# One PSUM layout for a whole two-layer block, kept rows and a turn moved in the Fourier stage, and queries turned in fp32r

## The chip, the core and the metric

The kernel runs on one core of one Trainium2 chip. The metric is device time in microseconds (us) of one execution. The time before is the median of three runs; beside it stands one profiled execution of the same kernel, from which every duration in this document is read.

## The reference, cut to what matters

A block of two layers works on 512 latent tokens of width 1024 (and, in the first layer, 256 context tokens). All of it is fp32.

- Each layer is: half-step SwiGLU FFN, a token mixer, half-step SwiGLU FFN. Every sub-layer first modulates its input (`x * (1 + scale) + shift`, from a conditioning vector) and ends with `layer_norm(ALPHA * x + gate * y) * g + b`.
- The mixer of layer 0 is attention with 16 query heads on 4 key heads of 64 columns, rotary positions, a band of 128 tokens to both sides, all context keys and one sink logit per head in the softmax.
- The mixer of layer 1 is a two-dimensional Fourier transform (over the 512 tokens, and over groups of 256 channels), its real part, and a projection.
- The context goes through the first FFN of layer 0 alone, and is used as keys and values.

```python
q, k, v = split(h @ w_qkv + b_qkv);  q, k = rope(q * scale), rope(k)
p = softmax([q k_window, q k_context, sink])          # per head, block of 128 queries
y = (p[window] @ v_window + p[context] @ v_context) @ w_o        # layer 0
y = real(fft2(h per channel group, axes=(token, channel))) @ w_o  # layer 1
x = layer_norm(ALPHA * x + gate * y) * g + b
```

## The kernel before

**Precision.** A product of two fp32 matrices is made of three products in fp32r, a 4-byte format of fewer mantissa bits. `split` (line 160) makes two parts of a matrix: `hi`, a rounded copy (ScalarE), and `lo`, what is left (VectorE). `mm3` (line 164) issues hi·hi, lo·hi and hi·lo into one PSUM accumulation. So each weight tile of 128x1024 costs a copy on ScalarE and a subtraction on VectorE (`wh`, `wl` in the profile), and for the weights whose output is gated also a product with the gate row (`wr<-wr,gr`).

**Buffers.** SBUF has a pool of 42 slots of 4 KB per partition (`slot`, line 135): weight rows as they land (`wr`), their parts, activations, probabilities, the LayerNorm rows. DMAs for weights go out on SyncE's queue, in order, as soon as a slot is free for them. PSUM has 8 banks of 512 fp32 columns. In the FFNs and the Fourier stage they are one pool of eight single banks (`open_banks(8)`); `bank` (line 144) takes one, and `bank2` (line 150) takes two of them. For the core of attention that pool is closed and another is opened, with four single banks and two tiles of two neighbouring banks (`open_banks(4, 2)`); afterwards that is closed and the eight come back. A tile of PSUM is given out again when the last instruction that reads it is through.

**Order.** TensorE and GpSimd run in the order in which the code emits. VectorE and ScalarE do so in the stretches between `nc.pin(True)` and `nc.pin(False)`; elsewhere a planner of the compiler orders their instructions. SyncE's DMAs are ordered by that planner too.

**An FFN half step** (`half_step`, line 566) runs 22 up pairs (`ffn_up`, line 410): for each, 48 matmuls into one `bank2`, a silu of one bank on ScalarE and a product with the other on VectorE. VectorE also folds the modulation vectors of later stages there (`mr`, `acc`), whose sums go through a single bank (`mp`). Then `project` (line 476) runs the down product into four `bank2` named `y`, one for each 128 tokens: the first part goes through the contraction for all four tiles together, and the last contraction tiles (`TAIL` = 4) go tile by tile, so that one token tile is finished after another. After each: `norm_stage` (VectorE), `scale_stage` (ScalarE), and for the tile before it `flip_stage` (line 351), eight turns of 128x128 on TensorE into a `bank2` named `tp`, then the affine part and the split of the next stage's input. The last tile's turns are left for the next stage, which calls them (`rest[0]`, the function `flip`) between its first products. The other function that `project` returns, `keeps` (line 533), makes the next residual: it loads two LayerNorm rows by DMA (`ln_rows`) and computes x·g + b for a token tile (`keep_stage`, line 389: two VectorE instructions of 128x1024).

**Attention** (line 925). `group` (line 1018) makes a product of 256 tokens by 512 columns into a `bank2` named `qkv`: three groups for keys and values, two for the first half of the queries, two for the second. Keys are turned by `kv_flip`. Queries of a group go through `q_post` (line 999): the bias for both token tiles (`qb`), then for each tile the rotary steps (`ra`) and `q_parts`, which puts each head's rounded part and its remainder side by side (`q`). `q_flip` (line 1006) turns them, eight 128x128 turns a token tile in fp32 into a `bank2` named `qt`, and ScalarE copies them out as `Q`. This happens eight times: four between the groups, four in steps 3 to 6 of the core. Between the last two groups, `whole` makes the scores of steps 0 and 1 with single banks. The core has 16 steps (key head by query tile); each makes the scores `s` of the step after next, turns probabilities (`pt`), and multiplies with values (`o`). A score tile has 512 or 640 columns; in the core it is one tile of two neighbouring banks. After the core the first product of `project` needs the split of the attention output (`uh`, `ul` from `oT`).

**Fourier** (line 1245). For each of four token tiles, two products `ab` of 12 matmuls of 258 columns go into one `bank2` each, and are split (`ah`, `al`) with an extra column copied to `nyq`. The turns of the last token tile of the FFN before (`rest[0]()`) are called behind both products of the second tile. Then for each of four channel groups 24 matmuls (`f`) go into two single banks, and VectorE and ScalarE combine them into `X`, which is split for the projection (`uh`, `ul`). That projection (8 contraction tiles) calls `keeps` after each of its first four contraction tiles: after the first one the rows are loaded and the first token tile is done, and so on.

L72 in the profile is the line of a helper through which all engine instructions are issued, so that groups are told apart by tile names.

Of the kernel before, what the change touches and what calls it, by code (L numbers as in the profile page):

```python
# [15 lines left out]
P = 128  # L16
# [3 lines left out]
BANK = 512  # L20
# [26 lines left out]
SLOTS = 42  # L47
EVAC_DVE = {4: (1,), 5: (1, 3)}
# [10 lines left out]
REACH_DFT = 9  # L59

# [32 lines left out]
class Banks:  # L93


    def __init__(self, tiles):
        self.tiles = tiles
# [7 lines left out]
class Emitter:  # L105
    def __init__(self, ctx, tc, ins, out):
        self.tc = tc
        self.nc = Engines(tc)
        self.ins = ins
        self.out = out  # L110
        self.pool = ctx.enter_context(tc.tile_pool(name="sb", bufs=1))
        self.dram = ctx.enter_context(tc.tile_pool(name="dram", bufs=2, space=bass.MemoryType.DRAM))
        self.open_banks(8)
        self.n = 0

    def open_banks(self, single, double=0):

        self.stack = ExitStack()
        self.psum, self.psum2 = (
            self.stack.enter_context(self.tc.tile_pool(name=nm, bufs=n, space=bass.MemoryType.PSUM)) if n else None  # L120
            for nm, n in ((f"ps{single}", single), (f"pd{single}", double))
        )
        self.bufs = single, double

    def close_banks(self):
        self.stack.close()
# [17 lines left out]
    def bank(self, nm="ps"):  # L144
        return self.psum.tile([P, BANK], F32, tag="ps", name=self.name(nm), bufs=self.bufs[0])

    def wide(self, nm):
        return self.psum2.tile([P, 2 * BANK], F32, tag="pd", name=self.name(nm), bufs=self.bufs[1])

    def bank2(self, nm="ps"):  # L150
        return Banks([self.bank(nm) for _ in range(2)])
# [4 lines left out]
    def turn(self, out, src):  # L156
        self.nc.tensor.transpose(out, src, self.ident)

# [251 lines left out]
    def ffn_up(self, pairs, h, N, quota, us, first=None, halves=False, late=None, held=None):  # L410
# [34 lines left out]
        for p in range(NPAIR):  # L445
# [10 lines left out]
            if first is not None and p in KEEP_AT:  # L456
                first[1](KEEP_AT.index(p))
# [18 lines left out]
    def project(self, w0, nf, stat, st, ntok, mid=None, keep=True, reach=REACH, each=None):  # L476
# [56 lines left out]
        def keeps(i=None):  # L533

            if keep:
                if not i:
                    st["rows"] = self.ln_rows(*st["ln"])
                for t in range(ntok) if i is None else (i,):
                    self.keep_stage(st, t)
# [61 lines left out]
    def head(self):  # L601
# [6 lines left out]
        banks = [self.bank("up") for _ in range(HEAD)]  # L608
        scratch = self.bank("ms")
        raws, xts, ws = {}, {}, {}  # L610
# [157 lines left out]
    def run(self):  # L768
# [128 lines left out]
        rest = self.project(w_fo, KC, fT, st, NT, each=keeps)  # L897
# [27 lines left out]
    def attention(self, w_kv, w_q, w_ao, h1, ch, rest):  # L925
# [52 lines left out]
        Q = {}  # L978

        def q_bias(tp, i, ps):  # L980
            qb = self.slot([P, 2, 512], F32, "qb")
            for tt in range(2):
                nc.vector.tensor_tensor(
                    qb[:, tt], ps[:, tt * 512 : (tt + 1) * 512], bq[:, i * 512 : (i + 1) * 512], ALU.add
                )
            return tp, i, qb, {}
# [5 lines left out]
        def q_parts(tp, i, qb, q2s, tt):  # L992
            q2 = self.slot([P, 8, 2, HD], F32, "q2")
            src = q2s[tt].rearrange("p (h d) -> p h d", d=HD)
            nc.vector.tensor_copy(q2[:, :, 0].bitcast(F32R), src)
            nc.vector.tensor_tensor(q2[:, :, 1], src, q2[:, :, 0], ALU.subtract)
            q2s[tt] = q2

        def q_post(tp, i, ps):
            q = q_bias(tp, i, ps)  # L1000
            for tt in range(2):
                q_rope(*q, tt)
                q_parts(*q, tt)
            return q

        def q_flip(tp, i, qb, q2s, tt):
            flip = self.bank2(nm="qt")
            for j in range(8):
                self.turn(flip[:, j * P : (j + 1) * P], q2s[tt][:, j].rearrange("p r d -> p (r d)"))
            q = self.slot([P, 8, P], F32R, "Q")  # L1010
            for h in range(2):
                src = flip[:, h * BANK : (h + 1) * BANK].rearrange("p (j q) -> p j q", q=P)
                nc.scalar.copy(q[:, 4 * h : 4 * h + 4], src)
            Q[2 * tp + tt, i] = q
# [3 lines left out]
        def group(tp, w0, last=False, between=None):  # L1018

            ps = self.bank2(nm="qkv")  # L1020
# [47 lines left out]
        def begin(n):  # L1068
# [9 lines left out]
            st = dict(g=g, b=b, total=total, nw=nw, tok=slice(b * P, (b + 1) * P))  # L1078
# [16 lines left out]
        def score(st, j):  # L1095
# [4 lines left out]
            total, nw, wide = st["total"], st["nw"], self.psum2 is not None  # L1100
# [96 lines left out]
        self.close_banks()  # L1197
        self.open_banks(4, 2)
# [40 lines left out]
        self.close_banks()  # L1239
        self.open_banks(8)  # L1240
# [4 lines left out]
    def fourier(self, w_t1, w_t2, w_fo, h, rest):  # L1245
# [11 lines left out]
        for t in range(NT):  # L1257
            pss = []
            for gp in range(FG // 2):
                ps = self.bank2(nm="ab")  # L1260
# [10 lines left out]
            if t == 1:  # L1271
                rest[0]()
            for gp in range(FG // 2):
# [5 lines left out]
                for gg in range(2):  # L1279
# [3 lines left out]
                    self.split(ah[:, t % 2, gg], al[:, t % 2, gg], src[:, : 2 * half])  # L1283
        ny = (self.slot([P, NT, P], F32R, "nyh"), self.slot([P, NT, P], F32R, "nyl"))
# [16 lines left out]
        for gr in range(FG):  # L1301
            ps, sine = (self.bank("f") for _ in range(2))
# [32 lines left out]
def kernel(ctx: ExitStack, tc: tile.TileContext, ins, out):  # L1335
    e = Emitter(ctx, tc, ins, out)
    e.run()
    e.close_banks()
# [110 lines left out]
```

## Time and profile before

| | |
|---|---|
| median of 3 runs (lowest, highest) | 1991.2 us (1990.84, 1992.42) |
| the profiled execution: its own time | 1992.59 us |
| its span, first to last instruction | 1990.8 us |
| mean granted TensorE clock | 0.999 |
| busy: TensorE, VectorE, ScalarE, GpSimd | 1971.8, 1277.0, 681.2, 73.4 us |
| DMA | 296 MB, 149 GB/s on average |
| attention up to its core | about 574 to 664 us of the span |
| the core of attention | 664 to 771 us |
| Fourier and its projection | 1548 to 1628 us |

How to read it: a group of instructions is shown by its engine and by `out<-in`, the names of the tiles. In the view of waits a line says which engine waited for which, the total, how often, and the longest. In the chain of waits each line is a start, a duration and what ran then. In the timeline a bracket behind an instruction is the time for which its engine stood idle before it, and what ended that. Records of matmuls overlap, since they are pipelined: their pace is read from their starts, or from the chain, not from their own duration.

### The profile page before, as it was taken

What the parts mean: (1) busy time and instruction counts of PE and PEld (TensorE: products, weight loads), DVE (VectorE), ACT (ScalarE), POOL (GpSimd) and SP (SyncE); (2) the same over time, 40 slices, a digit from 0 to 9 for tenths busy, and PEclk for the clock granted to TensorE, in tenths of its full rate; (3) what the DMA queues carried; (4) which work ended last, traced back from release to release, by engine and by line L of the source; (5) the groups of instructions that cost most, each with busy time, mean ns of one, the idle gap of its engine ahead of it and who ended that gap; (6) DMA issues with size and microseconds to landing.
All of it is one profiled execution on the core that took longest, in us unless ns stands there. A gap on an engine that the chain in (4) does not pass through costs nothing.

```text
span 1990.8 us, 25353 instructions
## 1 busy us (share of the span) xinstructions
PE 1971.8 (99%) x10124; PEld 1674.7 (84%) x10124; DVE 1277.0 (64%) x1713; ACT 681.2 (34%) x991; POOL 73.4 (4%) x138
## 2 busy tenths in 40 slices
PE   8999999999999999999999999999999999999998
PEld 7888888899888887988888888888888988888886
DVE  6569985598756775766658455664766873333744
ACT  3322243334533685422224232222333632212320
POOL 0000000000000460000000000000000000000000
PEclk9999999999999999999999999999999999999999
DMA  9756543388732013455543326554441333232411
GB/s 377 262 185 206 185 150 131 116 297 297 254 101 73 10 45 107 159 190 196 195 149 123 120 98 225 195 191 138 140 135 64 110 98 117 90 94 87 138 64 43
DMA packets 90198, 296.27 MB, mean 149 GB/s; under 512 B 17248, under 2 KB 17504, under 8 KB 90080
## 3 DMA queue, kind: packets, MB, share of 16 engines
q1 hardware_dynamic: 81792, 290.96, 43.0%
q10 hardware_dynamic: 8288, 3.70, 0.7%
q8 instruction: 79, 1.29, 0.3%
q14 instruction: 39, 0.32, 0.1%
HBM read 292.50 MB, written 2.13 MB: 148 GB/s over the span
## 4 chain that ended last, share of the span: by engine, by line
PE 96%; DVE 2%; DMA 1%; ACT 1%; issue 0%; DVEq 0%; POOL 0%; SPq 0%; ACTq 0%; POOLq 0%
PE up L72 54%; PE y L72 30%; PE qkv L72 4%; PE s L72 2%; PE pt L72 2%; PE o L72 1%; PE tp L72 1%; DVE wl L72 1%; DVE x L72 0%; PE ab L72 0%; DMA wr<-in_wi_head_dram 0%; PE qt L72 0%; DVE ul L72 0%; PE f L72 0%; DMA ln_b<-in_ln_b_col_dram 0%
## 5 line engine op out<-in xcount | busy, mean ns | idle before, releaser
L72 DVE TENSOR_TENSOR wl<-wr,wh 128x1024 fp32r<-128x1024 f32 (+1 forms) x359 | 429.1, 1217 | 90.9 <-ACT wh L72 55.3
L72 ACT CAST wh<-wr 128x1024 fp32r<-128x1024 f32 (+1 forms) x364 | 368.5, 1046 | 218.2 <-PE y L72 92.5
L72 PE MATMUL up<-hh,wh 128*128 128x512 f32 (+1 forms) x1152 | 429.6, 373 | 0.0
L72 PE MATMUL up<-hl,wh 128*128 128x512 f32 (+1 forms) x1152 | 428.3, 372 | 0.0
L72 PE MATMUL up<-hh,wl 128*128 128x512 f32 (+1 forms) x1152 | 428.1, 372 | 0.0
L72 PE MATMUL y<-wh,uh 128*128 128x512 f32 x920 | 302.7, 390 | 1.4 <-DVE oT L72 1.4
L72 ACT ACTIVATE sg<-up 128x512 f32<-128x512 f32 (+1 forms) x110 | 61.1, 555 | 703.5 <-PE up L72 703.5
L72 PE MATMUL y<-wh,ul 128*128 128x512 f32 x920 | 301.8, 389 | 0.0
L72 PE MATMUL y<-wl,uh 128*128 128x512 f32 x920 | 301.6, 389 | 0.0
L72 DVE TENSOR_TENSOR u<-up,sg 128x512 f32<-128x512 f32 (+1 forms) x110 | 70.1, 637 | 335.0 <-PE up L72 334.6
L72 PEld LDWEIGHTS up<-hl,wh 128*128 128x128 f32 x1152 | 217.1, 188 | 37.5
L72 PEld LDWEIGHTS up<-hh,wl 128*128 128x128 f32 x1152 | 217.2, 189 | 37.2
L72 PEld LDWEIGHTS up<-hh,wh 128*128 128x128 f32 x1152 | 217.2, 189 | 36.9
L72 PEld LDWEIGHTS y<-wh,uh 128*128 128x128 f32 x920 | 172.6, 188 | 37.1 <-DVE oT L72 1.8
L72 PEld LDWEIGHTS y<-wh,ul 128*128 128x128 f32 x920 | 172.8, 188 | 35.9
L72 PEld LDWEIGHTS y<-wl,uh 128*128 128x128 f32 x920 | 172.8, 188 | 35.5
L72 DVE SCALAR_TENSOR_TENSOR acc<-mr,silu_c,acc 128x1024 f32<-128x1024 f32 x147 | 186.1, 1280 | 1.4
L72 DVE TENSOR_TENSOR wr<-wr,gr 128x1024 f32<-128x1024 f32 x99 | 120.5, 1238 | 41.4 <-DMA wr<-in_wo_dram 22.3
L72 PE MATMUL up<-h0h,wh 128*128 128x512 f32 x352 | 139.1, 398 | 0.2 <-ACT h0h L72 0.2
L72 PE MATMUL up<-h0l,wh 128*128 128x512 f32 x352 | 136.4, 390 | 0.0
L72 PE MATMUL up<-h0h,wl 128*128 128x512 f32 x352 | 136.2, 390 | 0.0
L72 PE MATMUL up<-chh,wh 128*128 128x256 f32 x352 | 100.1, 284 | 0.0
(171 smaller groups left out, 2143.0 us busy)
## 6 DMA issues: line engine op xcount, KB each, us to landing
wr<-in_wi_dram SPq DMA_DIRECT2D x213, 512.0 KB, 4.4
mr<-in_mod_w_dram SPq DMA_DIRECT2D x144, 512.0 KB, 4.1
wr<-in_wo_dram SPq DMA_DIRECT2D x110, 512.0 KB, 3.9
m<-in_mod_head_dram SPq DMA_DIRECT2D x16, 512.0 KB, 8.1
wr<-in_wqkv_dram SPq DMA_DIRECT2D x12, 512.0 KB, 3.6
wr<-in_attn_wo_dram SPq DMA_DIRECT2D x8, 512.0 KB, 3.5
wr<-in_fourier_wo_dram SPq DMA_DIRECT2D x8, 512.0 KB, 3.5
wr<-in_wi_head_dram SPq DMA_DIRECT2D x8, 448.0 KB, 9.6
```

The lines of the kernel that those rows point to most:

```text
L72: ins = f(*args, **kw)
```

## The change

1. PSUM is divided once: four single banks (`SINGLES`) and two tiles of two neighbouring banks (`PAIRS`), from the first to the last instruction. `open_banks` and `close_banks` go. `bank2` gives a neighbouring two and two singles in turn, unless it is told which: `group` asks for a neighbouring two, `q_flip` for two singles. Steps 0 and 1 of the scores still use singles (`wide=n > 1`), now of four.
2. In `q_post` the bias, the rotary steps and the parts of one token tile are finished before the bias of the next.
3. `q_flip` turns in fp32r: the remainder is written as fp32r, and an identity in fp32r is made once by a ScalarE copy into a slot of its own. Eight flips of eight turns are concerned.
4. Fourier: the turns of the last token tile are called between the two products of the second tile instead of behind both.
5. Fourier: the LayerNorm rows are loaded behind the four token tiles, the first kept tile is computed in the first channel group, and the projection does the other three one contraction tile earlier each.

```diff
-        self.open_banks(8)
+        self.psum, self.psum2 = (
+            ctx.enter_context(tc.tile_pool(name=nm, bufs=n, space=bass.MemoryType.PSUM))
+            for nm, n in (("single", SINGLES), ("pair", PAIRS))
+        )
+        self.wide_next = True
...
-    def bank2(self, nm="ps"):
+    def bank2(self, nm="ps", wide=None):
+
+        if wide is None:
+            wide, self.wide_next = self.wide_next, not self.wide_next
+        if wide:
+            whole = self.wide(nm)
+            return Banks([whole[:, :BANK], whole[:, BANK:]], whole)
         return Banks([self.bank(nm) for _ in range(2)])
...
+    def turn_parts(self, out, src, ident):
+
+        self.nc.tensor.transpose(out.bitcast(F32R), src.bitcast(F32R), ident)
...
-                if not i:
+                if "rows" not in st:
                     st["rows"] = self.ln_rows(*st["ln"])
-                for t in range(ntok) if i is None else (i,):
+                for t in range(ntok) if i is None else i:
                     self.keep_stage(st, t)
...
-        rest = self.project(w_fo, KC, fT, st, NT, each=keeps)
+        rest = self.project(w_fo, KC, fT, st, NT, each=lambda f: keeps((f + 1,) if f + 1 < NT else ()))
...
-        def q_bias(tp, i, ps):
+        ident = self.slot([P, P], F32R, "ident_r")
+        nc.scalar.copy(ident, self.ident)
+
+        def q_bias(tp, i, ps, each=None):
             qb = self.slot([P, 2, 512], F32, "qb")
+            q = tp, i, qb, {}
             for tt in range(2):
                 nc.vector.tensor_tensor(
                     qb[:, tt], ps[:, tt * 512 : (tt + 1) * 512], bq[:, i * 512 : (i + 1) * 512], ALU.add
                 )
-            return tp, i, qb, {}
+                if each is not None:
+                    each(q, tt)
+            return q
...
-            nc.vector.tensor_tensor(q2[:, :, 1], src, q2[:, :, 0], ALU.subtract)
+            nc.vector.tensor_tensor(q2[:, :, 1].bitcast(F32R), src, q2[:, :, 0], ALU.subtract)
...
-            flip = self.bank2(nm="qt")
+            flip = self.bank2("qt", False)
             for j in range(8):
-                self.turn(flip[:, j * P : (j + 1) * P], q2s[tt][:, j].rearrange("p r d -> p (r d)"))
+                self.turn_parts(flip[:, j * P : (j + 1) * P], q2s[tt][:, j].rearrange("p r d -> p (r d)"), ident)
...
-            ps = self.bank2(nm="qkv")
+            ps = self.bank2("qkv", True)
...
-            total, nw, wide = st["total"], st["nw"], self.psum2 is not None
+            total, nw, wide = st["total"], st["nw"], st["wide"]
...
-        self.close_banks()
-        self.open_banks(4, 2)
...
             for gp in range(FG // 2):
+                if t == 1 and gp == 1:
+                    rest[0]()
                 ps = self.bank2(nm="ab")
...
-            if t == 1:
-                rest[0]()
...
+        rest[1](())
         ny = (self.slot([P, NT, P], F32R, "nyh"), self.slot([P, NT, P], F32R, "nyl"))
...
-            ps, sine = (self.bank("f") for _ in range(2))
+            ps, sine = self.bank2("f").tiles
...
+            if gr == KEEP_DFT:
+                rest[1]((0,))
```

In the head of the kernel, which sums the first seven up columns in seven banks beside a scratch bank, four of the seven now come from the two neighbouring twos.

More of the change, by code (lines that the diff above doesn't have):

```diff
@@ L47 @@
 SLOTS = 42
+SINGLES = 4
+PAIRS = 2
 EVAC_DVE = {4: (1,), 5: (1, 3)}
@@ L59 @@
 REACH_DFT = 9
+KEEP_DFT = 0
 class Pinned:
@@ L93, with __init__ @@
 class Banks:
-    def __init__(self, tiles):
-        self.tiles = tiles
+    def __init__(self, tiles, whole=None):
+        self.tiles, self.whole = tiles, whole
     def __getitem__(self, at):
@@ L112, in __init__ @@
         self.dram = ctx.enter_context(tc.tile_pool(name="dram", bufs=2, space=bass.MemoryType.DRAM))
-        self.open_banks(8)
-        self.n = 0
[L116 to L126, printed above, removed]
+        self.psum, self.psum2 = (
[3 more added lines that the diff above has]
+        self.wide_next = True
+        self.n = 0
     def name(self, s):
@@ L144, in bank @@
     def bank(self, nm="ps"):
-        return self.psum.tile([P, BANK], F32, tag="ps", name=self.name(nm), bufs=self.bufs[0])
+        return self.psum.tile([P, BANK], F32, tag="ps", name=self.name(nm), bufs=SINGLES)
     def wide(self, nm):
-        return self.psum2.tile([P, 2 * BANK], F32, tag="pd", name=self.name(nm), bufs=self.bufs[1])
-    def bank2(self, nm="ps"):
+        return self.psum2.tile([P, 2 * BANK], F32, tag="pd", name=self.name(nm), bufs=PAIRS)
+    def bank2(self, nm="ps", wide=None):
[4 more added lines that the diff above has]
+            return Banks([whole[:, :BANK], whole[:, BANK:]], whole)
         return Banks([self.bank(nm) for _ in range(2)])
@@ L456, in ffn_up @@
             if first is not None and p in KEEP_AT:
-                first[1](KEEP_AT.index(p))
+                first[1]((KEEP_AT.index(p),))
             if p == p_late:
@@ L607, in head @@
         hi, lo = h[0][0], h[0][1]
-        banks = [self.bank("up") for _ in range(HEAD)]
         scratch = self.bank("ms")
+        singles = [self.bank("up") for _ in range(SINGLES - 1)]
+        banks = [*singles[:2], *(b for _ in range(PAIRS) for b in self.bank2("up", True).tiles), singles[2]]
         raws, xts, ws = {}, {}, {}
@@ L995, in q_parts, with rest @@
             nc.vector.tensor_copy(q2[:, :, 0].bitcast(F32R), src)
-            nc.vector.tensor_tensor(q2[:, :, 1], src, q2[:, :, 0], ALU.subtract)
+            nc.vector.tensor_tensor(q2[:, :, 1].bitcast(F32R), src, q2[:, :, 0], ALU.subtract)
             q2s[tt] = q2
         def q_post(tp, i, ps):
-            q = q_bias(tp, i, ps)
-            for tt in range(2):
+            def rest(q, tt):
                 q_rope(*q, tt)
                 q_parts(*q, tt)
-            return q
+            return q_bias(tp, i, ps, rest)
         def q_flip(tp, i, qb, q2s, tt):
-            flip = self.bank2(nm="qt")
+            flip = self.bank2("qt", False)
             for j in range(8):
-                self.turn(flip[:, j * P : (j + 1) * P], q2s[tt][:, j].rearrange("p r d -> p (r d)"))
+                self.turn_parts(flip[:, j * P : (j + 1) * P], q2s[tt][:, j].rearrange("p r d -> p (r d)"), ident)
             q = self.slot([P, 8, P], F32R, "Q")
@@ L1077, in begin @@
             total = nw + CTX
-            st = dict(g=g, b=b, total=total, nw=nw, tok=slice(b * P, (b + 1) * P))
+            st = dict(g=g, b=b, total=total, nw=nw, wide=n > 1, tok=slice(b * P, (b + 1) * P))
             st["segs"] = [(0, CTX, cx), (CTX, nw, win)] if b == NT - 1 else [(0, nw, win), (nw, CTX, cx)]
@@ L1238, in attention @@
         divide(work.pop(n_steps - 1))
-        self.close_banks()
-        self.open_banks(8)
         nc.pin(False)
@@ L1337 @@
     e.run()
-    e.close_banks()
 def _constants():
```

## The prediction

> **What bounds the kernel now.** I read the page first, then the waits of TensorE alone, then the chain of waits and the timeline around each of them.
>
> ```profile
> PE 1971.8 (99%) x10124; PEld 1674.7 (84%) x10124; DVE 1277.0 (64%) x1713; ACT 681.2 (34%) x991; POOL 73.4 (4%) x138
> ```
>
> TensorE is busy for all but 19 us of a span of 1990.8, so the change can win only by fewer or shorter TensorE instructions, or by taking away one of its waits. These are all that the view of waits has for it:
>
> ```profile
> PE ms L72 <- DMA m<-in_mod_head_dram: 6.7, 1, 6.7
> PE y L72 <- DVE oT L72: 1.4, 1, 1.4
> PE tp L72 <- ACT x L72: 0.9, 1, 0.9
> PE s L72 <- DVE qb L72: 0.8, 1, 0.8
> PE ab L72 <- DVE al L72: 0.7, 1, 0.7
> PE qt L72 <- DVE q L72: 0.4, 1, 0.4
> PE up L72 <- ACT h0h L72: 0.2, 1, 0.2
> ```
>
> The first is the load at the start, which the change doesn't touch; the five in the middle, 4.2 us together, are each in a place that it does. The rest of the idle time is the first instructions and VectorE's last LayerNorm. So the whole question is some 4 us of waits, the price of 64 turns, and what two pools of PSUM bring in new waits.
>
> **The first query tile.** The chain there runs through VectorE:
>
> ```profile
> 623.99 1.20 DVE qb L72 x2
> 627.68 0.70 DVE q L72
> 628.52 1.06 PE qt L72 x8
> 635.06 0.87 PE qt L72 x8
> ```
>
> Two biases stand ahead of the first tile's rotary steps; with the second one moved behind, that tile is ready 0.6 us sooner (half of 1.20). TensorE lost 0.4 by its row, a little more by the starts. I take 0.5, and 0.4 to 0.6. The second tile gets all its VectorE work in the same total, and its turns come 6.5 us after the first tile's (635.06 against 628.52). The moved bias also holds its PSUM tile four VectorE instructions longer, about 3 us, while the next group that asks for this tile is two groups later. Price nothing.
>
> **The turns.** Eight in fp32 take 0.87 us where nothing stands before them: 109 ns each, 64 of them. The trace has no fp32r matmul with fewer than 256 columns. Its nearest rows are the fp32r chains of 258 columns (f) and 512 columns (qkv), and, for the load of the other operand, a fp32 matmul of one column (ms):
>
> ```profile
> 1561.40 2.88 PE f L72 x24
> 650.55 5.47 PE qkv L72 x24
> 28.66 0.84 PE ms L72 x8
> L72 PEld LDWEIGHTS qt<-ident,q x64: 138/140/143, 628.5 to 711.7; 128*128 128x128 f32 x64
> L72 PEld LDWEIGHTS f<-wh,ah 128*128 128x128 f32 x32 | 6.1, 192 | 0.0
> ```
>
> 2.88/24 is 120 ns and 5.47/24 is 228, so 254 columns more cost 108 ns, 0.425 a column. Down this line a turn of 128 columns is 120 − 130 × 0.425 = 65 ns, a gain of 44 × 64 = 2.8 us. By the column alone (128/258 of 120) it is 60 ns and 3.1 us. On the other side, a matmul of one column still takes 105 ns (0.84/8), which I read as the load of 128x128; if a turn in fp32r waits for such a load it stays at 105 and the gain is 0.3. And a load of an fp32r operand is recorded with 192 ns where that of an fp32 turn has 140: were all of this 52 ns to show, a turn would take 161 and the change would lose 3.3. I take 65: the turn's moving operand becomes what the two chains move, and its load, shorter than the others in the record, is that of a turn. The identity costs one ScalarE copy on an engine at 34%, off the path.
>
> The Trainium skill (TensorE: Matmul & The Clock Gate, "LDWEIGHTS (loading the stationary operand)") gives a load as its columns over 1.2 ns, 107 ns for 128; by it no turn falls below 107, and the gain would be some 0.1 us. The one-column row agrees with it; the 140 against 192 of the loads doesn't say that every load is alike. That case is the first rival.
>
> **Four singles where there were eight.** In the second of the two early score steps each head takes two banks, so heads 2 and 3 need the banks of heads 0 and 1 back:
>
> ```profile
> 657.17 0.48 DVE L72 CUSTOM_DVE_ANT_0 p<-s,mask,part 128x256 f32<-128x256 f32 x1
> 658.35 0.48 DVE L72 CUSTOM_DVE_ANT_0 p<-s,mask,part 128x256 f32<-128x256 f32 x1
> 657.98 0.41 PE L72 MATMUL s<-KC,Q 128*128 128x256 f32 x2
> ```
>
> The last pair of matmuls began at 657.98. Of four banks it would get the one that VectorE reads until 658.35 + 0.48 = 658.83, and it starts at 658.95 with 0.1 for the signal: 1.0 us later. TensorE has its next group right behind, with no slack, so this is 1.0 on the path (0 if the planner finds a free bank, 1.2 at most). In the FFNs a tile still comes back after three others, two products of 48 matmuls (11 us each at 228 ns) being the least between; the two reads of a tile take 0.7 us each by the bias rows of the same size. Price nothing there; that cover would have to shrink tenfold.
>
> **No closing and opening.** Two of the waits sit exactly where the pools are changed:
>
> ```profile
> 658.39 5.45 PE qkv L72 x24
> 663.87 0.70 DVE qb L72
> 664.61 0.85 PE s L72 x4
> 768.28 1.13 DVE ul L72
> 770.47 0.43 DVE oT L72
> 770.94 32.95 PE y L72 x144
> ```
>
> The first score of the core waits for a bias read of a group's tile, which has nothing to do with its data. In the new kernel it takes the neighbouring two that the group before last has left. TensorE was done at 658.39 + 5.45 = 663.84, so 0.8 goes. What is late next is VectorE: that bias still precedes its first score. But the second score needs the tile of this bias only after the first score and four turns, about 1.3 us, and the bias takes 0.7. After the core, the first y waits for the last division `oT`, though its own operand `ul` is ready at 769.41. In the new kernel it takes a neighbouring two, free since the last scores; 770.94 falls to about 769.6, so 1.3 goes of the 1.4. The second y takes two of four singles and follows six matmuls later, past all reads but that division's.
>
> **The turns in the Fourier stage.** Here the pools work against the move.
>
> ```profile
> 1554.32 1.50 ACT L72 ACTIVATE ht<-tp,B,G 128x128 f32<-128x128 f32 x4 [1.09 <-PE tp L72]
> 1554.76 1.37 DVE L72 TENSOR_SCALAR ht<-tp,G,B 128x128 f32<-128x128 f32 x4 [0.80 <-PE tp L72]
> 1557.80 0.34 DVE al L72
> 1558.28 3.12 PE ab L72 x24
> ```
>
> The turns start 12 matmuls sooner, 1.45 us at 120 ns. ScalarE then begins 1.09 earlier and VectorE 0.80, their idle times; the split behind them waits for ScalarE's copy, so the first `al` of the second token tile, which ended at 1558.14, ends at about 1557.05. Before, the fourth token tile's first product waited for it (0.7). Now count the calls of `bank2`: an FFN half step makes 22 up, 4 y and 4 tp, an even number, so each starts alike; its y are two, singles, two, singles, the tp two, singles, two, and the Fourier stage goes on with singles: ab singles, two; ab singles, tp two, ab singles; third tile two, singles; fourth two, singles. The third tile's second product so needs the singles of the second tile's first product, one product earlier than the old kernel needed that read. It is due 1.45 before 1557.6 (1558.28 − 0.7), at 1556.15, and starts at 1557.2: a stall of 1.05 for one of 0.7. That is +0.4 (the whole 0.7 gained if a free bank is found, 1.0 lost if the fourth tile waits too).
>
> **The kept rows.**
>
> ```profile
> 1566.27 0.41 DVE L72 TENSOR_TENSOR X<-edge,zero 1x255 f32<-1x255 f32 x1
> 1569.04 1.42 DVE L72 TENSOR_TENSOR X<-f,qs 128x256 f32<-128x256 f32 x4 [2.36 <-ACT qs L72]
> L72 DVE TENSOR_TENSOR x<-x,ln_g_row 128x1024 f32<-128x1024 f32 x4 | 4.9, 1216 | 0.0
> 1607.92 1.09 PE tp L72 x8
> 1568.51 0.80 SPq L182 DMA_DIRECT2D wr<-in_fourier_wo_dram  x2
> 1572.95 0.33 SPq L317 DMA_DIRECT2D ln_g_row<-in_ln_g_row_dram  x1
> ln_b_row<-in_ln_b_row_dram SPq DMA_DIRECT2D x6, 512.0 KB, 5.1
> ```
>
> One kept tile is two instructions of 1.22, 2.4 us. It goes into an idle stretch of VectorE of 2.36, so it costs 0.1 there; without that cover it would be 2.4. From the projection, where VectorE ran without a pause up to the LayerNorm whose result `x` the turns at 1607.92 waited for, 2.4 is taken away. TensorE's wait of 0.9 is shorter than that, and goes; I count 0.9. The two DMAs go out earlier on SyncE, past the last two weight loads of the projection (1568.51), and their two slots are gone earlier for these. Those weights are used behind four contraction tiles of 24 matmuls, 22 us at 228 ns each, so a few microseconds later cost nothing. Nor do the rows, as long as they have landed by 1566.7 (1566.27 + 0.41), when VectorE reaches the moved pair.
>
> **Sum.** −0.5 − 2.8 + 1.0 − 0.8 − 1.3 + 0.4 − 0.9 = −4.9 us. The profiled execution took 1992.59 (its span and 1.8 around it), so its like would take 1987.7; it lay 1.4 above the median of 1991.2, and against that the forecast is 1986.3.
>
> **Rivals.**
>
> The turn stays at its load. For it: the one-column row of 105 ns; against it: the turn's shorter load record. Then 0.3 is gained of 2.8, and the time is 1988.8.
>
> A wait only makes room for the next. Where TensorE comes sooner at the query tile, the core's first scores, the first y and the last turns, the next VectorE result might be just as late, since VectorE is the engine that each of them waits for already. Then the 3.5 us of these four terms go, with the 2.8 of the turns kept against the 1.4 of new stalls: 1989.8. Against it: in each place the data is ready before the wait ends.
>
> The LayerNorm rows come late (the slower side). VectorE takes its instructions in order there, so the moved pair would hold up every `X` behind it. If the rows still got no slot before 1572.95 they would land at 1578.1, 11.4 us past 1566.7; the chain in this stretch runs through VectorE, so it would end 11.4 − 2.4 = 9.0 later in place of 0.9 sooner: 1986.3 + 9.9 = 1996.2. It decides from a landing at 1573 on, where the rest of the gain is eaten. For it: SyncE issued the rows only then, after waiting for a slot. Against: in the code they now ask for slots ahead of those that filled the pool.
>
> The turn gets dearer, 161 ns by the load records: 6.1 more than the forecast, 1992.4.
>
> **How the numbers follow.** Forecast 0.52, load-bound turn 0.25, next wait 0.11, late rows 0.08, dearer turn 0.04. The forecast's own range is 1983.9 (turn at 60, no new stalls: 0.3 + 1.0 + 1.1 better) to 1988.7 (no gain at the query tile and the first y, 1.8, and the Fourier stall at its worst, 0.6). The range for 8 in 10 goes from 1983.9 to 1992.4, which leaves out the late rows and tails. A measurement of this kernel can tell about 0.2% (4 us) from no change, so faster is below 1987.2 and slower above 1995.2. Faster: four fifths of the forecast and a tenth of the load-bound turn, 0.44. Slower: the late rows, and 0.03 for stalls of the four singles that I haven't seen, 0.11. Same: 0.45.
>
> **What would show it.** Turns: `qt` with eight in 0.5 us, not 0.87. Waits of TensorE: no `s <- qb`, no `y <- oT`, no `tp <- x`, no or a tiny `qt <- q`; new, an `s <- p` of 1 us near 658, and an `ab <- al` of about 1 us that comes a product earlier. Rows: `ln_g_row` issued before 1560. It is wrong if TensorE's waits behind the start exceed 4.2 us in all, if a `bank2` of the FFNs appears among them, or if VectorE stands idle for a DMA in the Fourier stage.

## The result, and the profile after

The changed kernel is slower: 1998.24 us in the median of six runs (1996.74 to 2000.10) against 1991.62 (1990.84 to 1992.58); the ratio is 1.0033, with a 95% interval of 1.0023 to 1.0044. The forecast was 1986.3, with a range up to 1992.4. The profiled execution took 1997.73 us, with a span of 1995.6.

First the busy row of the page after, then the waits of TensorE after (engine, what it waited for, total, times, longest), without the load at the start and one of 0.2.

```profile
PE 1973.8 (99%) x10124; PEld 1673.6 (84%) x10124; DVE 1277.0 (64%) x1713; ACT 681.7 (34%) x992; POOL 73.6 (4%) x138
```

```profile
PE ab L75 <- DVE al L75: 2.9, 2, 2.4
PE y L75 <- DVE u L75: 1.9, 1, 1.9
PE tp L75 <- ACT z L75: 1.5, 1, 1.5
PE up L75 <- DVE wl L75: 0.8, 1, 0.8
PE s L75 <- DVE qb L75: 0.4, 1, 0.4
PE tp L75 <- ACT x L75: 0.3, 1, 0.3
```

Three of the waits that I wanted gone are gone: `y <- oT`, `qt <- q`, and the late `tp <- x` (the one here is at another place); of `s <- qb` half is left. In their stead stand three in the FFNs and at the attention's first turns (`u`, `z`, `wl`), where I had priced nothing, and in the Fourier stage `ab <- al` has grown from 0.7 to 2.9.

Where the time went is best seen by stages. For the table I took, in two traces, the start of the same TensorE instruction at nine places and subtracted; each row shows by how much the stage became longer (+) or shorter (−) than before. The first row comes from the start, which differs between executions and belongs to no edit: TensorE's load lands at 6.70 us before and 6.35 after, and its early products run slower up to 15.04 and 11.94, where the record of the granted clock begins (the first seven `up <- h0h,wh` take 3.3 us before and 2.1 after). In the second column my own forecast stands for the stages. "Up to" a stage's first y, first turns or first f means up to the start of that instruction.

| stage (us) | forecast | after | division alone | all but the division |
|---|---|---|---|---|
| start, first FFN, up to its first turns | 0 | −1.54 | −0.01 | −1.68 |
| context FFN, up to its first y | 0 | +1.07 | +0.57 | 0.00 |
| its projection, the attention's first turns and groups | 0 | +1.78 | +1.72 | −0.01 |
| queries and early scores | −0.9 | −0.10 | +0.98 | −1.09 |
| last group and core, up to the first y behind it | −3.5 | −2.48 | −1.81 | −0.65 |
| the attention's projection, first FFN behind it, up to its first turns | 0 | +0.28 | +0.29 | +0.01 |
| second FFN behind it (layer 1), up to its first turns | 0 | +3.87 | +1.35 | 0.00 |
| Fourier, up to the first f | +0.4 | +3.18 | +2.53 | −0.87 |
| rest of Fourier, its projection | −0.9 | −0.91 | +0.04 | −0.95 |

Without the first row the column "after" adds up to +6.7, and the medians lie 6.6 apart. The last two columns are two of the experiments. With all but the division no stage behind the first becomes longer by more than 0.01; with the division alone the same stages lose. So what I missed comes with the division of PSUM. ScalarE shows how. The silus of an FFN in the timeline of ScalarE, before and after (start, duration, instruction; in brackets how long ScalarE had been idle, and what it waited for):

```profile
1299.74 0.60 ACT L72 ACTIVATE sg<-up 128x512 f32<-128x512 f32 x1 [8.40 <-PE up L72]
1310.62 0.60 ACT L72 ACTIVATE sg<-up 128x512 f32<-128x512 f32 x1 [8.40 <-PE up L72]
1321.50 0.60 ACT L72 ACTIVATE sg<-up 128x512 f32<-128x512 f32 x1 [8.40 <-PE up L72]
```

```profile
1304.23 0.60 ACT L75 ACTIVATE sg<-up 128x512 f32<-128x512 f32 x1 [13.84 <-PE up L75]
1309.67 0.60 ACT L75 ACTIVATE sg<-up 128x512 f32<-128x512 f32 x1 [2.96 <-PE up L75]
1325.99 0.60 ACT L75 ACTIVATE sg<-up 128x512 f32<-128x512 f32 x1 [13.84 <-PE up L75]
```

Before, a silu came every 10.88 us: it reads the first bank of a product, which is done when the first 24 of 48 matmuls are. After, the gaps alternate, 5.44 and 16.32: every second silu comes 5.44 us late, which is 24 matmuls of 227 ns. These are the products in a neighbouring two. That is one tile of the program, and a reader of its first half waits for the last matmul into its second half. Two singles are two tiles.

The silu itself is in no hurry. But ScalarE works in order, and behind one of these silus stands the gate row of the projection: the column `gs`, its DMA out (`there`), and the DMA back (`gr`), which ScalarE issues when the first has landed. The end of layer 1's first FFN (which the expectations call the second FFN of layer 1), in the timeline of ScalarE before and after:

```profile
1389.71 0.31 ACT L72 ACTIVATE gs<-mod 128x8 f32<-128x8 f32 x2
1389.95 1.01 ACTq L72 DMA_DIRECT2D there<-gs  x2
1402.24 0.82 ACTq L72 DMA_DIRECT2D gr<-there  x2
```

```profile
1391.83 0.60 ACT L75 ACTIVATE sg<-up 128x512 f32<-128x512 f32 x1 [13.84 <-PE up L75]
1394.44 1.01 ACTq L75 DMA_DIRECT2D there<-gs  x2
1406.55 1.85 ACTq L75 DMA_DIRECT2D gr<-there  x2
1408.45 1.05 ACT L75 CAST uh<-u 128x1024 fp32r<-128x1024 f32 x1 [10.59 <-DMA there<-gs]
```

The silu at 1391.83 holds up the two weight copies and the column behind it; the row leaves 4.5 us later (1394.44 against 1389.95), or 5.44 later counted from TensorE's own instructions, which are 0.95 earlier in this trace. VectorE, which multiplies the weights with the row, begins that work 3.65 us later:

```profile
1408.42 1.23 DVE L72 TENSOR_TENSOR wr<-wr,gr 128x1024 f32<-128x1024 f32 x1 [9.80 <-DMA gr<-there]
```

```profile
1412.07 1.23 DVE L75 TENSOR_TENSOR wr<-wr,gr 128x1024 f32<-128x1024 f32 x1 [13.84 <-DMA gr<-there]
```

The first y products then catch up with VectorE, and TensorE waits 1.9 us for `u`. The wait has a sequel. The granted clock (third number from the end) and TensorE's busy time (the number behind the comma) in three windows after, the first of which holds the wait:

```profile
1428.47:1431.88 3.41, 1.55 (x7) 0.98 (x6) 3.41 (x5) 2.76 (x3) 0.00 (x0) 1.00 0.55 154
1431.88:1435.29 3.41, 3.41 (x9) 2.68 (x8) 3.41 (x5) 0.18 (x1) 0.00 (x0) 0.50 0.24 53
1435.29:1438.70 3.41, 3.41 (x16) 2.82 (x15) 3.37 (x4) 2.96 (x3) 0.00 (x0) 1.00 0.64 259
```

Behind the wait the clock stood at 0.50 for 3.41 us. At half the clock that loses 1.7 us more, so the 3.87 of this stage are 1.9 of waiting, 1.7 of a slow clock and 0.3 of small gaps.

The second thing that a shared tile does is seen in the Fourier stage. The turns `tp` have two halves: ScalarE takes the first, VectorE the second. After, from the timelines of ScalarE, VectorE and TensorE:

```profile
1558.12 1.52 ACT L75 ACTIVATE ht<-tp,B,G 128x128 f32<-128x128 f32 x4
1559.68 1.37 DVE L75 TENSOR_SCALAR ht<-tp,G,B 128x128 f32<-128x128 f32 x4 [0.98 <-ACT ht L75]
1562.91 0.36 PE L75 MATMUL ab<-wh,hh 128*128 128x258 f32 x1 [2.38 <-DVE al L75]
```

Here VectorE begins when ScalarE is through with its four (1558.12 + 1.52 = 1559.64). Before, on two singles, it began 0.44 behind ScalarE's start (1554.76 against 1554.32, in the prediction's rows). In all, the view of waits has VectorE standing 10.7 us, nine times, for ScalarE's `ht` after, and no such row before.

```profile
DVE ht L75 <- ACT ht L75: 10.7, 9, 2.0
ACT nyq L75 <- DVE al L75: 2.0, 3, 0.8
```

So readers on two engines are served one after the other when their banks are one tile. The Trainium skill (PSUM — Partial Sum Buffer, "PSUM bank collisions raise a hardware error") asks for such an order within one bank. The two halves here lie in two banks, so that it is the program's tile, and not that rule, that orders them.

### The profile page after: what moved, and what is told of

Read it like the earlier page. It is cut to its first block, busy times and chain, and to the rows that moved or that the text cites. A ratio compares the mean times of both kernels' runs of the same rounds, so it can differ in the third digit from the quotient of the medians.

```text
span 1995.6 us, 25306 instructions
## 1 busy us (share of the span) xinstructions
PE 1973.8 (99%) x10124; PEld 1673.6 (84%) x10124; DVE 1277.0 (64%) x1713; ACT 681.7 (34%) x992; POOL 73.6 (4%) x138
## 3 DMA queue, kind: packets, MB, share of 16 engines
q8 instruction: 79, 1.29, 0.3%
## 4 chain that ended last, share of the span: by engine, by line
PE 94%; DMA 2%; DVE 2%; ACT 1%; issue 0%; SPq 0%; POOL 0%; DVEq 0%; ACTq 0%; POOLq 0%
PE up L75 52%; PE y L75 31%; PE qkv L75 4%; PE s L75 2%; PE o L75 2%; PE pt L75 2%; DMA there<-gs 1%; PE tp L75 1%; DMA m<-in_mod_head_dram 1%; PE f L75 1%; DVE wl L75 0%; PE qt L75 0%; DVE wr L75 0%; DMA gr<-there 0%; DVE bs L75 0%
## 5 line engine op out<-in xcount | busy, mean ns | idle before, releaser
L75 DVE SCALAR_TENSOR_TENSOR x<-x,y 128x512 f32<-128x512 f32 x48 | 32.5, 680 | 107.8 <-PE y L75 107.3
```

Source lines behind the costliest of these rows:

```text
L75: ins = f(*args, **kw)
```

## The experiments

My theory (U in the expectations) is that the loss comes from waits that hold for a whole tile. One rival (R) is that fewer tiles rotate, so that banks come back late; another (M) is that the moved turns in the Fourier stage are the loss.

**1. The division alone.** The kernel before with edit 1, and none of the others.

```diff
-        self.open_banks(8)
+            for nm, n in (("single", SINGLES), ("pair", PAIRS))
...
+            whole = self.wide(nm)
+            return Banks([whole[:, :BANK], whole[:, BANK:]], whole)
```

> The kernel before with the division of PSUM alone (no turns in fp32r, no finishing by tile, nothing moved in the Fourier stage). Theory U (one tile, one wait): a reader of the first half of a neighbouring two waits for the last matmul into its second half, so in every second up product the silu comes 5.4 us later; the gate rows, issued behind a silu on ScalarE, come late with it. Then this kernel has the losses of the changed one in the FFNs (about 1.0 in the context FFN, 3.8 in the second FFN of layer 1 in order of execution), about 1.8 at the attention's first turns and 1.0 in the early scores, against 1.35 gained at the first y behind the core: 5 to 6 us slower than before, about 1997. Theory M (the moved turns in the Fourier stage are what costs): about 2 us slower than before at most, near 1993.

Measured: 1998.41 us, ratio 1.0033 (1.0021 to 1.0046), as slow as the changed kernel with all its edits. By stages it is the third column of the table: 0.57 and 1.72 around the context FFN, 1.35 at layer 1's FFN, and 2.53 in the Fourier stage without any moved turns. M falls. U's total was 1.4 short: it had nothing on the Fourier stage, and more on layer 1's FFN than this execution shows.

**2. All but the division.** The changed kernel with the old pools.

```diff
+        self.open_banks(8)
...
-            ps = self.bank2("qkv", True)
+            ps = self.bank2("qkv")
```

> The changed kernel with the old pools put back (eight singles, and four and two for the core), all other edits kept. Theory U: the silus come at 10.9 us intervals again, no wait of TensorE for a gated weight is longer than before; left are the gains: turns 1.8, first query tile 0.5, kept rows 0.9, and the moved turns between 0.7 gained and 0.5 lost. 1988 to 1989, faster than both. Theory M: the moved turns cost 3 in this kernel too, which eats the gains: 1991 to 1992.

Measured: 1988.27 us, ratio 0.9982 (0.9973 to 0.9991): faster than both. All waits of TensorE behind the start, but for one of 0.2 at 19 us, are these:

```profile
PE y L75 <- DVE oT L75: 1.4, 1, 1.4
PE s L75 <- DVE qb L75: 0.8, 1, 0.8
```

The moved turns gain 0.87 here and cost nothing; it takes eight singles for that. This kernel is also where the turns in fp32r are read. From the timeline of TensorE before and here, the second group of turns and the product behind it, and from the view of the tile `qt` here, the load:

```profile
634.90 1.03 PE L72 MATMUL qt<-ident,q 128*128 128x128 f32 x8
635.69 0.48 PE L72 MATMUL qkv<-wh,hh 128*128 128x512 f32 x1
```

```profile
632.60 0.79 PE L75 MATMUL qt<-ident_r,q 128*128 128x128 f32 x8
633.23 0.46 PE L75 MATMUL qkv<-wh,hh 128*128 128x512 f32 x1
```

```profile
L75 PEld LDWEIGHTS qt<-ident_r,q x64: 137/140/143, 626.3 to 708.3; 128*128 128x128 f32 x64
```

From start to start, eight turns between two groups take 0.63 (79 ns each) where fp32 took 0.79 (99 ns); in the core it is 0.71 for 0.85. The load is the same 140 ns as before. The prediction's 0.87 was the chain's figure for the same turns, 0.08 more than these starts.

**3. The up products on singles.** The changed kernel, with the up products in two singles each (but the first one or two of an FFN), so that they rotate in four banks.

```diff
-                ps = self.bank2(nm="up")
+                ps = self.bank2("up", p == 0)
```

> The changed kernel, but the up products take two singles each (but for the context FFN's first and the first two where a FFN begins by halves, which alternate as they did); the neighbouring twos stay for y, tp, ab, f and the groups. The up products so rotate in four banks, where the changed kernel had eight. Theory U: the silu comes when the first 24 matmuls are done, ScalarE's wait for the gate column's DMA falls from 32.7 us to about 10, and the losses of the FFNs go: 4 to 5 us faster than the changed kernel, about 1993.5. Rival R (too few banks in rotation): with half the banks the up products wait for their readers; TensorE shows waits for u or sg in every FFN, and the time rises above 1998.

Measured: 1994.79 us, ratio 1.0016 (1.0007 to 1.0025), 3.4 us faster than the changed kernel. The context FFN's stage went from +1.07 to +0.03 and layer 1's from +3.87 to +0.13: the whole loss of the FFNs is gone with half the banks. R falls. Of ScalarE's waits:

```profile
ACT uh L75 <- DMA there<-gs: 8.4, 2, 5.2
```

It was 32.7 in four after. The total gained less than the 4 to 5 expected because the Fourier stage, which the edit doesn't touch, came out at +4.68 instead of +3.18. There the clock dipped in this execution:

```profile
1556.86:1560.27 3.41, 1.27 (x10) 1.30 (x11) 3.23 (x8) 2.37 (x13) 0.00 (x0) 1.00 0.00 0
1560.27:1563.68 3.41, 3.41 (x18) 3.41 (x17) 1.15 (x3) 1.26 (x8) 0.00 (x0) 0.50 0.02 5
```

Half the clock for 3.41 us is 1.7 us, behind a wait of 2.38 for `al`. After the same wait at the same place the changed kernel's own execution kept its clock.

**4. The turns put back.** The changed kernel with `rest[0]()` behind both products of the second token tile again.

```diff
-                if t == 1 and gp == 1:
-                    rest[0]()
...
+            if t == 1:
+                rest[0]()
```

> The changed kernel with the turns of the last token tile put back behind both products of the second tile in the Fourier stage. If the stalls there (0.3, 0.5, 2.4 us) come from the move, since the splits of earlier products queue on ScalarE and VectorE behind the turns' chain while their banks are asked for one product sooner: 2.5 to 3.2 us faster than the changed kernel, about 1995.3, and the waits of TensorE for al fall from 2.9 to about 0.7. If they come from the norm of the last tile being late by the tile's shared wait: the waits stay about as long wherever the turns stand, and the time within 0.7 us of 1998.

Measured: 1995.73 us, ratio 1.0019 (1.0010 to 1.0028), 2.5 us faster than the changed kernel. But only 0.7 of it lies in the Fourier stage (+2.52 instead of +3.18); the rest is layer 1's FFN, where this execution had a shorter wait for `u` (1.3) and no dip of the clock behind it (+1.71 instead of +3.87). The waits for `al` didn't fall to 0.7:

```profile
PE ab L75 <- DVE al L75: 2.3, 2, 1.7
PE tp L75 <- DVE al L75: 0.4, 1, 0.4
```

So the time agreed with the first expectation by accident, and the stage with the second: the stalls don't come from the place of the turns. The division alone has them too (+2.53). The late norm that the second expectation names is in the traces. VectorE's last instruction for the norm of the last token tile, before and after:

```profile
1549.96 0.16 DVE L72 SCALAR_TENSOR_TENSOR nm<-mv,rs 128x1 f32<-128x1 f32 x1
```

```profile
1554.10 0.16 DVE L75 SCALAR_TENSOR_TENSOR nm<-mv,rs 128x1 f32<-128x1 f32 x1
```

TensorE starts the turns of the first token tile at 1534.30 before and 1537.18 after. Counted from there, `nm` comes at 15.66 before and 16.92 after. In all six kernels with the divided PSUM it is 16.91 or 16.92, in all five with eight singles 15.65 or 15.66. So VectorE comes into the Fourier stage 1.3 us late, wherever the turns stand. The third y tile is a neighbouring two, and its norm begins only when the whole tile is done.

**5. A late silu without any change of PSUM, first try.** The kernel before; in every second up product the second half is made first, so that the half for the silu is ready last.

```diff
-            for half in range(2):
+            for half in ((1, 0) if p >= 2 and p % 2 == 0 else (0, 1)):
```

> The kernel before, with its eight single banks, but in every second up product (the even ones from the third on) the half that VectorE multiplies is made first and the half for the silu second. No bank is added, taken or joined; only the silu of these products comes 5.4 us later, where the changed kernel has it. Theory U (the late silu and the gate row behind it are the loss in the FFNs): it pays what the changed kernel paid at the ends of the FFNs, about 1.1 at the context FFN and 3.9 at the second FFN of layer 1: about 1996.5. Rival R (the loss is in how banks come back): no difference to before, 1991.8.

Measured: 1997.04 us, ratio 1.0027 (1.0017 to 1.0036). The total is the one expected, its parts aren't: +3.69 at the context FFN, +1.59 at layer 1's. The edit does more than I wanted: the weight that is now used first is still split second, and TensorE waits for it.

```profile
PE up L72 <- DVE wl L72: 2.3, 3, 1.1
PE y L72 <- DVE u L72: 1.3, 1, 1.3
```

**6. The same, with the weights in the order of their use.** The two weights of such a pair are swapped where they are loaded, and the silu takes the second half.

```diff
-                for s in range(2):
+                for s in (1, 0) if p >= 4 and p % 2 == 0 else (0, 1):
...
+            a, b = (512, 0) if p >= 4 and p % 2 == 0 else (0, 512)
+            nc.scalar.activation(sg, ps[:, a : a + N], AF.Silu)
+            nc.vector.tensor_tensor(u, ps[:, b : b + N], sg, ALU.mult)
```

> The kernel before, eight single banks, with the two weights of the even up pairs (from the fifth on) swapped in their order of loading and use, so that the silu takes the second half of such a product: the same lateness of the silu as in the run with swapped halves, but the weights are split in the order in which they are used. Theory U: TensorE's waits for split up weights in the context FFN (2.3 in that run) fall to the changed kernel's 0.8, and both losses show: about 1.1 at the context FFN's end and 1.5 to 3.9 at the second FFN of layer 1's end (the upper end with the dip of the clock behind the wait), 1994.5 to 1997. Rival R: 1991.8.

Measured: 1993.68 us, ratio 1.0010 (1.0001 to 1.0019), 2.0 us slower than before, a little under the lower end expected. Eight single banks, no tile shared, and yet the context FFN's stage is longer by 0.67 and layer 1's by 1.60, all other stages within 0.1. The signature is that of the changed kernel:

```profile
PE y L72 <- DVE u L72: 1.3, 1, 1.3
PE up L72 <- DVE wl L72: 0.4, 1, 0.4
ACT uh L72 <- DMA there<-gs: 23.2, 3, 10.2
```

So the late silu alone makes the gate row late and TensorE wait. What the changed kernel pays beyond that at layer 1 (3.87 against 1.60) is 0.6 more of waiting and the 1.7 of the clock; at the context FFN (1.07 against 0.67) it is 0.4 more of waiting for `wl`.

**7. Other tiles for the same banks.** The changed kernel; the neighbouring twos go to the odd up products, the context's two y tiles swap kinds, and in the Fourier stage both copies of ScalarE come ahead of both subtractions of VectorE.

```diff
-                ps = self.bank2(nm="up")
+                ps = self.bank2("up", p % 2 == 1)
...
+        self.wide_next = ntok > 2
...
-                    self.split(ah[:, t % 2, gg], al[:, t % 2, gg], src[:, : 2 * half])
+                    nc.scalar.copy(ah[:, t % 2, gg], src[:, : 2 * half])
+                for gg in range(2):
+                    src = pss[gp].tiles[gg]
+                    nc.vector.tensor_tensor(
```

> The changed kernel, PSUM divided as there, with three edits at places that can be read apart. First, the neighbouring twos go to the odd up products instead of the even ones, so that the silu ahead of the gate column in ScalarE's order reads a single: by theory U the losses at the ends of the context FFN (1.1) and of the second FFN of layer 1 (3.9) fall to 0.5 at most each; by rival R they stay, since as many banks rotate. Second, in the context FFN's projection the first token tile takes two singles and the second the neighbouring two: if the late start of the norm on a shared tile makes the turns wait (1.5 for z), that wait goes, 1.7 less. Third, in the Fourier stage ScalarE's copies of both halves of a product come ahead of VectorE's two subtractions (they alternated): if readers on two engines are served one after the other on a shared tile, ScalarE's waits for al (2.0 in three) go there, and the front of the stage gets 0.5 to 1.5 shorter; if not, it stays. Sum: 1990.5 to 1992 under U with all three, 1998 if none holds.

Measured: 1992.39 us, ratio 1.0003 (0.9994 to 1.0012): 5.9 us of the 6.6 are recovered with PSUM divided as before. The FFNs lose 0.04 and 0.12 (from 1.07 and 3.87), the attention's first turns 0.80 (from 1.78), the front of the Fourier stage 2.32 (from 3.18).

```profile
PE ab L75 <- DVE al L75: 2.2, 2, 1.7
PE qkv L75 <- DVE kvb L75: 0.5, 1, 0.5
PE tp L75 <- ACT x L75: 0.3, 1, 0.3
```

No `u`, no `wl`, no `z`; ScalarE's waits for `al` are gone as well. Of the 1.5 that the first turns no longer wait for `z`, 0.5 went into a new wait for `kvb`. As many banks rotate as in the changed kernel, so in the FFNs and at the first turns only the kind of tile under a reader can be the cause; in the Fourier stage the order of the copies changed as well.

**8. The moved turns on two singles.** The run before this one, with a neighbouring two first in the Fourier stage, so that the kinds of all its tiles swap.

```diff
+        self.wide_next = True
         for t in range(NT):
             pss = []
```

> The run with odd pairs, with one thing turned round in the Fourier stage: its products begin with a neighbouring two instead of two singles, so that the moved turns of the last token tile land on two singles instead of a neighbouring two. If what is left of the loss there (2.3 us from the last y turns to the first f, where eight singles gained 0.9) comes from VectorE standing behind ScalarE on the tile of the turns: VectorE's half of the affine part starts 1.5 us sooner, TensorE's longest wait for al falls from 1.7 to below 0.5, and the time by 1.2 to 2 us, to about 1990.7. If it comes from which product's banks come back when, the wait moves to another product and the time stays at 1992.4, give or take 0.5.

Measured: 1993.43 us, ratio 1.0007 (0.9998 to 1.0016), 1.0 us slower than the seventh. VectorE's half did come sooner, at 0.86 behind ScalarE's start instead of 1.61:

```profile
1552.89 1.57 ACT L75 ACTIVATE ht<-tp,B,G 128x128 f32<-128x128 f32 x4
1553.75 1.35 DVE L75 TENSOR_SCALAR ht<-tp,G,B 128x128 f32<-128x128 f32 x4
```

```profile
PE ab L75 <- DVE ht L75: 1.2, 1, 1.2
PE y L75 <- DVE X L75: 1.1, 1, 1.1
PE ab L75 <- DVE al L75: 0.9, 1, 0.9
```

The wait for `al` fell from 1.7 to 0.9, and two others took its place: an early `ab` now wants the banks of the turns before it, and the projection behind the stage waits for `X`. The front is 1.99 longer than before (2.32 in the seventh), and the rest 0.59 longer where the seventh had −0.79. Both readings that I had offered hold in part. The division costs 2 to 3 us in this stage, and with eight singles none of it is there. The 1.3 us by which VectorE comes late from the norm (experiment 4) are ahead of all tiles that this edit swaps, and stay as they were; how much of the loss is theirs, and which of the shared tiles makes up the rest, is not settled.

**9. Pools in another order.** The kernel of the second experiment; for the core, the two neighbouring twos are opened ahead of the four singles.

```diff
-        self.psum, self.psum2 = (
+        self.psum2, self.psum = (
```

> The changed kernel with the old pools, as in the run with all but the division, but for the core the two neighbouring twos are opened ahead of the four singles, so that they lie in other banks. If a new tile waits only for the last reader of the banks that it lies in: behind the core the first y gets banks of a score tile, free since the last scores, and TensorE's wait of 1.4 for oT goes; at the core's start the first score either finds a free bank (0.8 less) or waits as now. 1986 to 1987. If opening a pool waits for everything in the old one: 1988.3 as there.

Measured: 1988.23 us, ratio 0.9983 (0.9974 to 0.9991), the same as the second. Both waits stay, with the 1.4 and 0.8 of the second. Either a new pool waits for the last reader of the whole old one, or the first tiles still lie on the same banks; the trace shows no addresses, so this is open. These two kernels remain the fastest, 3.5 us below before and 10 below the changed kernel.

## Why the prediction was wrong, point by point

- **First query tile, −0.5:** right. TensorE's wait for `q` went; the start of the first `qt` moved by −0.46 in the second experiment (the stage's −1.09 less the turns).
- **Turns, −2.8:** the mechanism was right, the size wrong. 64 turns gained 1.1 by their starts (0.59 among the groups, 0.54 in the core), and the two stages became 0.63 and 0.65 shorter. A turn takes 79 to 89 ns and not 65. I started from the chain's 109 ns, where the starts say 99 to 106, extrapolated to 65 from the length of the moving rows alone, and took the turn's shorter load record as a sign that its load wouldn't show. That load stayed at 140 ns while the turn got 20 ns shorter. The load-bound rival (105) was wrong as well. In another section than the one that I weighed, the Trainium skill (TensorE: Matmul & The Clock Gate, "Back-to-back issue gap") has pairs of a load and a matmul of 128 columns come every 81 ns; the trace agrees with that, at 79 between groups.
- **Four singles in the early scores, +1.0:** right, 0.98 in the division alone. It shows in the starts of the scores; the view of waits has no row `s <- p`, which I had expected.
- **First score of the core, −0.8:** gained at the first score, and half of it lost at the second. The first score now follows the last product without a wait (664.90 after). The 0.4 that is left is the second score's, which takes the last group's tile. For that one I counted a single bias of 0.7. After, both biases begin behind the whole product, at 665.10, and take 1.29 together; before, the first of them ran at 661.11, during the products of the second token tile. It is the same lateness of a first reader as in the FFNs. Over the core some 0.5 was gained (the −1.81 of the division alone less 1.35 at the y).
- **First y behind the core, −1.3:** right; its wait of 1.4 is gone.
- **Kept rows, −0.9:** right, −0.91 with two pools and −0.95 with eight singles.
- **Turns moved in the Fourier stage, +0.4:** wrong, +3.18. "Now count the calls of `bank2`" asked whose banks come back when, and took the readers' times from before. On shared tiles the readers are later: they begin with the whole tile and go one after the other, and VectorE comes into the stage 1.3 late from the norm. With eight singles the move gains 0.87, the end that I gave as "0.7 gained if a free bank is found"; with the division this stage loses 2.5 without the move.
- **The FFNs, "Price nothing there":** the step that failed. I showed that a tile comes back in good time and never asked when a tile may be read first. The runs showed that a first reader waits for the whole tile: every second silu came 5.44 us late, and with it the gate row and the weights (experiments 3, 6 and 7), and the context's norm began late (`z`, experiment 7). It cost 1.07, 1.78 and 3.87 in three stages, 6.7 us together (1.7 of them the clock), as much as the kernel became slower; the terms that I had named net out at −0.3 (−0.5 − 1.3 + 1.0 − 0.5 − 1.3 + 3.2 − 0.9).
- **Rivals:** none had this. "A wait only makes room for the next" came nearest, but in the wrong places. The late LayerNorm rows didn't happen. What I had named as a sign of being wrong is what occurred: TensorE's waits behind the start exceed 4.2 us (8.0 by the rows above and one of 0.2), and the FFNs are among them; but TensorE waits there for operands (`u`, `wl`), not for a `bank2` that comes back late, which is what I had in mind.

## What to carry to other kernels

When two buffers become one, ask two questions and not one: when does it come back, and when may its first reader start. A pipeline that lives on reading one half while the other is being written, or on two engines reading one half each, loses that when the halves become one tile. An engine that works in order passes such a lateness on to whatever stands behind it: here the silu itself could come 5 us later without loss, and the DMA behind it could not.

## What was unexpected of the hardware

A wait of TensorE of some 2 us can cost nearly as much again. Behind 1.86 us of idling at layer 1's FFN the granted clock stood at 0.50 for 3.41 us, and the y products lost 1.7 us to it; behind 2.38 us in the Fourier stage of the third experiment it did the same. The same 2.38 in the changed kernel had no such sequel, nor had waits up to 1.7 behind the start in any run. The Trainium skill (TensorE: Matmul & The Clock Gate, "What's actually happening") puts the fall behind an idle window of about 3.4 us; here less than 2 sufficed, and not each time.

The traces show what the sequel hangs on. Between its changes the clock stayed full for 1419.94 and 556.37 us in the changed kernel and for 1546.24 in the third experiment, which is 416, 163 and 453 times 3.413 us. So the clock changes on a grid of 3.41 us, and where that grid lies differs between executions. On it, the 2.38 us in the changed kernel fall across a border, with TensorE idle for 1.04 us of one window and 1.34 of the next (3.41 less its busy time):

```profile
1558.16:1561.57 3.41, 2.37 (x18) 2.01 (x17) 2.32 (x6) 2.59 (x7) 0.00 (x0) 1.00 0.00 0
1561.57:1564.98 3.41, 2.07 (x17) 2.10 (x18) 2.82 (x9) 2.68 (x17) 0.00 (x0) 1.00 0.00 0
```

The windows ahead of the two falls, shown above, hold 1.86 and 2.14 us of idling. From the first full clock to the last product, no other window of the eleven traces has more than 1.72 us (experiments 1 and 4, in the Fourier stage), and none of them was followed by half the clock. In this case, then, the limit lay between 1.72 and 1.86 us of idling in one window; two falls are few to rest a rule on.
